# Weight parts, x and y at multiples of 512 bytes in SBUF, in a fused decoder layer on one core

## Chip, cores, metric

The kernel runs on one core of a Trainium2 chip. The metric is the device time of one execution in microseconds. PE, ACT, DVE, POOL and SP are the engines for matrix products, activations, vector operations, general work and DMA issues.

## What is computed

One decoder layer with four mixers, and a final RMSNorm:

```python
D_MODEL = 4096; SEQ = 256; DEPTH = 1; D_BRANCH = 1024
def hybrid_layer(x, norm_w, w_in, ..., w_out):
    h = rms_norm(x, norm_w)
    proj = jnp.einsum('bsd,de->bse', h, w_in)          # 4096 x 13328
    (rq, rk, rv, rg, mq, mk, mv, mg, sz, sxbc, sdt, lx, lg) = jnp.split(proj, ...)
    y_ret  = retention(rq, rk, rv, ret_gn_w) * silu(rg)
    y_moba = moba_attention(mq, mk, mv) * silu(mg)
    y_ssm  = mamba2_ssd(sz, sxbc, sdt, ...)
    y_lru  = rg_lru(lx, ...) * silu(lg)
    y = jnp.concatenate([y_ret, y_moba, y_ssm, y_lru], axis=-1)
    return x + jnp.einsum('bse,ed->bsd', y, w_out)     # 4096 x 4096
# then rms_norm(x, final_norm_w)
```

All inputs are float32. Each large product is made of three matmuls in the type float32r, from parts: an operand a is split into a high part (a rounded to float32r) and a low part (a minus the high part), and the kernel adds high x high, low x high and high x low.

## The kernel before, in words

**Chunks.** The weights come in chunks, as a rule two k-tiles (`KC = 2`, 256 rows of the weight) by 512 columns, in the order in which they are used. The columns of `w_in` are put into 25 groups (`GROUPS`). The first group has 1040 columns (`rv` and `sdt`) and is read one k-tile at a time, 32 chunks, each with the x rows it needs; the other 24 have 512 columns and 16 chunks each; the output projection has 8 column tiles of 512 and 16 chunks each. `load(n)` issues the DMA of chunk n on SP into one of four `raw` tiles (`RAW = 4` chunks ahead). `split(n)` (lines 145 to 160) makes `whi` on ACT (line 159) and `wlo` on DVE (line 160), two chunks ahead (`SPL = 2`), three tiles of each. For the last output tile some chunks are kept in six `hhi`/`hlo` tiles.

**Matmuls.** `products` (lines 669 to 674) makes three matmuls for one half e of the 256 rows: line 672 high x of the activations with `whi`, line 673 low x with `whi`, line 674 high x with `wlo`. The activations' parts are the weights that PE holds (128x128 out of a tile `xT` of 512 columns: high e=0, high e=1, low e=0, low e=1), and `whi`/`wlo` stream through as the moving operand, 512 columns at a time. In the first group each k-tile's 1040 columns are cut by `CUTS` into 504, 280 and 256 columns, in three pairs of accumulators (two `pm` pairs, one `pb` pair). The output projection does the same in `mms` (lines 727 to 735) with `yhl`, the split outputs of the mixers, in `xT` tiles too: per chunk of two k-tiles six matmuls for e=0 and then six for e=1. In the last output tile the second half of the rows is done in two halves of 256 columns.

**Everything between.** The mixers' own work is cut into short functions in a list, `todo`, and one of them (`slot()`) goes between two chunks. Their scratch tiles `t1` are six tiles of 512 columns that are handed out in turn. `softplus` (lines 261 to 275) has five small tiles of its own in the `const` pool, for `dt` (32 columns, in `ssd_dt`) and for `lam` (8 columns, in `lru_lam`). `lru_gate` (lines 493 to 510) multiplies split weights `lwh`, `lwl` (held by PE) with a split `r1` tile (moving), 12 matmuls of 256 columns for a pair of heads. A row of bf16 matmuls on a tile of zeros (line 659) runs at the start.

**Where tiles lie.** Pools are laid one behind the other along the bytes of a partition, in the order in which they are opened; a pool's tiles lie one behind the other, each of its own size. The `const` pool begins at byte 16512 and takes 7712, so `xT` begins at 24224, which is 160 past a multiple of 512; a tile of 2048 bytes keeps that offset. A `raw`, `whi` or `wlo` tile has 1040 columns (`RW`), 4160 bytes, which is 64 past a multiple of 512. By this and the new pools of the change, the offsets (address modulo 512) are:

| tile | before | with the change |
|---|---|---|
| `xT` (split x, later split y), each of its four parts | 160 | 0 |
| `whi`, three buffers, each of two k-tiles | 416, 480, 32 | 0, 0, 0 |
| `wlo`, three buffers | 96, 160, 224 | 0, 0, 0 |
| `whi` in the first group: second and third cut | whi + 480 and whi + 64 | 0 and 0 |
| `hhi`, `hlo`, `rs`, `fw`, `xres` | 448 (`rs` 288) | 0 |
| `raw`, four buffers | 160, 224, 288, 352 | 0, 64, 128, 192 |
| `lwh`, `lwl` of the gates | 384 | 352 |
| `r1` of the gates | 320 | 288 |
| `t1` | 320 | 288 |

The pairs `whi`/`wlo` are used in turn: 480/160, then 416/96, then 32/224.

Of the kernel before, what the change touches and what calls it, by code (L numbers as in the profile page):

```python
# [11 lines left out]
F32 = mybir.dt.float32  # L12
# [5 lines left out]
P = 128  # L18
# [3 lines left out]
KC = 2  # L22
XW = S + 1
SPL, RAW, HOLD, WARM = 2, 4, 6, 34
RW = 1040
CUTS = ((0, 504), (504, 784), (784, 1040))
NCH = KT // KC
EPS = 1e-6

# [27 lines left out]
NO = D // 512  # L57
# [34 lines left out]
def tile_kernel(ctx: ExitStack, tc: tile.TileContext, t: dict):  # L92
# [4 lines left out]
    cp = ctx.enter_context(tc.tile_pool(name="const", bufs=1))  # L97
    xp = ctx.enter_context(tc.tile_pool(name="xp", bufs=KT))
    wp = ctx.enter_context(tc.tile_pool(name="wp", bufs=1))
    pm = ctx.enter_context(tc.tile_pool(name="pm", bufs=4, space=PSUM))  # L100
    pb = ctx.enter_context(tc.tile_pool(name="pb", bufs=4, space=PSUM))
    br_stack = ExitStack()
    sp = br_stack.enter_context(tc.tile_pool(name="sp", bufs=2))
# [9 lines left out]
    for gi, (what, cols) in enumerate(GROUPS):  # L113
        w = len(cols)
# [10 lines left out]
    def b4():  # L125
        return br.tile([P, 4, S], F32, name="b4", bufs=4)

    def load(n):
        if n >= len(chunks):
            return  # L130
        where, src, kt, nk, w = chunks[n]
        raw = wp.tile([P, RW], F32, name="raw", bufs=RAW)
        if where == "x":
            c, k = divmod(kt, KC)
            xraws[n] = b4().rearrange("p a b -> p (a b)")
            nc.sync.dma_start(out=xraws[n][:, :XW], in_=t["xt"][c][:, k * XW:(k + 1) * XW])
        if n == 0:

            for i, (a, b) in enumerate(CUTS):
                (nc.sync if i else nc.scalar).dma_start(out=raw[:, a:b], in_=src[:, a:b])  # L140
        else:
            nc.sync.dma_start(out=raw[:, :nk * w], in_=src)
        raws[n] = raw

    def split(n):
        if n >= len(chunks):
            return
        where, _, kt, nk, w = chunks[n]
        if where == "x":
            split_x(xraws.pop(n))  # L150
        raw = raws.pop(n)
        c = kt // KC
        pool, tag, bufs, size = wp, "w", SPL + 1, RW
        if where == "last" and c % (SPL + 1 + HOLD) > SPL:
            pool, tag, bufs, size = holds[0], "h", HOLD, KC * 512
        hi = pool.tile([P, size], F32R, name=tag + "hi", bufs=bufs)
        lo = pool.tile([P, size], F32R, name=tag + "lo", bufs=bufs)
        for a, b in CUTS if n == 0 else ((0, nk * w),):
            A.copy(hi[:, a:b], raw[:, a:b])  # L159
            V.tensor_tensor(lo[:, a:b], raw[:, a:b], hi[:, a:b].bitcast(F32), ALU.subtract)  # L160
        parts[n] = (hi, lo)
# [5 lines left out]
    def pcol(name, i=0, n=1):  # L167
        return par[:, PCOL[name][0] + i:PCOL[name][0] + i + n]

    xT, holds = [], []  # L170

    def split_x(raw):
        x = xp.tile([P, 512], F32R, name="xT")
        r, g = raw[:, 0:S], raw[:, S:XW]
        A.activation(x[:, 0:256], r, AF.Copy, scale=g)  # L175
        V.scalar_tensor_tensor(x[:, 256:512], r, g, x[:, 0:256].bitcast(F32), op0=ALU.mult, op1=ALU.subtract)  # L176
        xT.append(x)
# [48 lines left out]
    st = {}  # L226

    def t1(name="t1"):
        return sp.tile([P, 512], F32, name="t1", bufs=6)

    lent = itertools.cycle([12, 14])

# [25 lines left out]
    def to_qk(tk, qk, u):  # L258
        A.copy(qk[:, 2 * u:2 * u + 2, :], turned(tk, u).rearrange("p (a b) -> p a b", a=2))

    def softplus(x, n, tag):

        a, e, s, q, p = (cp.tile([P, n], F32, name=f"sp_{tag}{i}") for i in range(5))
        V.scalar_tensor_tensor(a, x, -1.0, x, op0=ALU.mult, op1=ALU.min)
        A.activation(e, a, AF.Exp)
        V.tensor_scalar(s, e, 2.0, None, op0=ALU.add)
        V.reciprocal(s, s)
        V.tensor_tensor(s, s, e, ALU.mult)
        V.tensor_tensor(q, s, s, ALU.mult)
        V.tensor_scalar(p, q, 1.0 / 17, None, op0=ALU.mult)  # L270
        for k in range(15, 1, -2):
            V.scalar_tensor_tensor(p, p, 1.0 / k, q, op0=ALU.add, op1=ALU.mult)
        V.scalar_tensor_tensor(p, p, 1.0, s, op0=ALU.add, op1=ALU.mult)
        V.tensor_scalar(a, x, 0.0, None, op0=ALU.max)
        V.scalar_tensor_tensor(x, p, 2.0, a, op0=ALU.mult, op1=ALU.add)
# [27 lines left out]
    def norm_mm(hl, n):  # L303
        ps = pb.tile([P, 512], F32, name="pb")
        for k in range(2):
            T.matmul(ps[:, :n * S], ones_r, hl[k][:, :n * S], start=k == 0, stop=k == 1)
        r = t1()
        A.activation(r[:, :n * S], ps[:, :n * S], AF.Sqrt, bias=epsc[:, 0:1], scale=1.0 / 256)
        V.reciprocal(r[:, :n * S], r[:, :n * S])
        return r  # L310
# [81 lines left out]
    dt = cp.tile([P, 2, 16], F32, name="dt")  # L392
# [3 lines left out]
    selr = cp.tile([48, 16], F32R, name="selr")  # L396

    def ssd_dt():
        softplus(dt.rearrange("p a b -> p (a b)"), 32, "dt")
        V.memset(da, 0.0)  # L400
        ea = cp.tile([P, 16], F32, name="ea")
        A.activation(ea, pcol("alog", 0, 16), AF.Exp)
        for k in range(2):
            V.scalar_tensor_tensor(da[:, k, 0:16], dt[:, k, :], -1.0, ea, op0=ALU.mult, op1=ALU.mult)
            V.tensor_copy(da[:, k, 32:48], da[:, k, 0:16])
        V.tensor_copy(selr, con[0:48, C_SEL:C_SEL + 16])
# [63 lines left out]
    lam8 = cp.tile([P, 8], F32, name="lam8")  # L470

    def lru_lam():
        V.tensor_scalar(lam8, pcol("lam", 0, 8), -1.0, None, op0=ALU.mult)
        softplus(lam8, 8, "lam")
        V.tensor_scalar(lam8, lam8, -8.0, None, op0=ALU.mult)

    def lru_w(n):
# [60 lines left out]
    def after(what, ps):  # L538
        name, i = what
        if name == "rv":  # L540
            st["v"] = [br.tile([P, 1024], F32, name="v") for _ in range(2)]
            for j, (a, b) in enumerate(CUTS):
                n = min(b, 1024) - a
# [69 lines left out]
        elif name == "lx":  # L613
            tk = rows_of(ps)

            def f(e):
                n = 4 * i + e
                lru_w(n)
                conv(piece("lxT", e), "lcw", n, pcol("lcb", n), ych(Y_LRU + n))

            def both(*fs):
                for g in fs:
                    g()

            split, ugate, scan = ([lambda n=4 * i + e, g=g: g(n) for e in range(4)] for g in
                                  (lru_split, lru_gate, lru_scan))
            todo.extend([None, lambda: turn(tk, 0, "lxT"), lambda: f(0), lambda: f(1), lambda: turn(tk, 1, "lxT"),
                         lambda: both(split[0], split[1]), lambda: f(2), lambda: both(ugate[0], ugate[1]),
                         lambda: f(3), lambda: both(split[2], split[3]), None, lambda: both(ugate[2], ugate[3]), None,
                         lambda: both(scan[0], scan[1]), lambda: both(scan[2], scan[3])])  # L630
        else:
            base = {"sz": Y_SSM, "rg": Y_RET, "mg": Y_MOBA, "lg": Y_LRU}[name]
            todo.extend(gate(ps, base + 4 * i))
            if name == "sz" and i == 1:
                todo.append(None)
                norm_units(Y_SSM, "snw")
# [17 lines left out]
    for n in range(RAW):  # L654
        load(n)
# [4 lines left out]
    for n in range(SPL):  # L660
        split(n)
# [14 lines left out]
    n, c0, ps = 0, 0, None  # L676
    while chunks[n][0] in ("x", "in"):
        _, _, k0, nk, w = chunks[n]
        if k0 == 0:
# [3 lines left out]
            if c0 == 1:  # L683
                ps += [pb.tile([P, 512], F32, name="pb") for _ in range(2)]
        split(n + SPL)
        load(n + RAW)
        hi, lo = parts.pop(n)
        for k in range(nk):
            kt = k0 + k
            for j, (a, b) in enumerate(CUTS if c0 == 1 else ((0, w),)):  # L690
                for e in range(2):
# [27 lines left out]
    br_stack.close()  # L719
    fp = ctx.enter_context(tc.tile_pool(name="fp", bufs=1))  # L720
    holds.append(fp)
    rs = [fp.tile([P, D], F32, name=f"rs{k}") for k in range(2)]
    fss = fp.tile([P, 2, NO + 1], F32, name="fss")
    m = fp.tile([P, 2], F32, name="fm")
    fr = fp.tile([P, 2], F32, name="fr")

    def mms(ps, e, c, p, c0=0, c1=512):
        hi, lo = p
# [37 lines left out]
    for o in range(NO):  # L766
# [11 lines left out]
        for c in range(NCH):  # L778
            split(n + SPL)
            load(n + RAW)  # L780
            held[c] = parts.pop(n)
            mms(ps[0], 0, c, held[c])
            n += 1
            if c == NCH - 1:
                finish(o, 0, ps[0], xres[0], fw)
            if c >= lag:
                p = held.pop(c - lag)
                for a, b in ((0, 256), (256, 512)) if lag else ((0, 512),):
                    mms(ps[1 + a // 256], 1, c - lag, p, a, b)
# [59 lines left out]
```

## Time and profile before

| what | us |
|---|---|
| median of 3 runs (lowest, highest) | 1601.29 (1600.91, 1603.0) |
| profiled execution: its own time | 1602.49 |
| profiled execution: span from first to last instruction | 1600.7 |
| PE busy | 1586.9 |
| DVE busy | 856.8 |
| ACT busy | 749.2 |

The profile was taken in one execution. Its span goes from the first instruction to the last; the execution's own time is 1.8 us longer. A PE row of the timeline tells when a matmul starts and how long it lasts until its results are there; the next one starts before that, so the spacing of two starts is what a matmul costs on PE.

### The profile page before, as it was taken

Reading aid. Unit: us, or ns where it says so; the run is one execution under the profiler, and the core shown is the slowest. Engines: PE = TensorE matmul, PEld = TensorE weight load, DVE = VectorE, ACT = ScalarE, POOL = GpSimd, SP = SyncE. Lnnn points to the kernel's source line nnn. Section 1 sums busy time; section 2 is a strip of 40 time slices with the busy share of each in tenths; the row PEclk is TensorE's granted clock in tenths of the full one; section 3 lists DMA queues with packets and bytes.
Section 4 is the critical chain, followed back from the end, with each engine's and each line's share of the span. In section 5 each row is a group of like instructions: output and inputs, shape, how many; then the busy total and the mean of one; then the engine's idle time right before and its main releaser. Section 6 shows DMA issues by size and latency. Waiting matters only on the chain.

```text
span 1600.7 us, 19179 instructions
## 1 busy us (share of the span) xinstructions
PE 1586.9 (99%) x7356; PEld 1302.5 (81%) x7356; DVE 856.8 (54%) x1024; ACT 749.2 (47%) x936; POOL 19.2 (1%) x39
## 2 busy tenths in 40 slices
PE   9999999999999999999999999999999999999997
PEld 8988888888887778888888888888888888888886
DVE  5564444475556644444457667444456444545454
ACT  5654444454445434444448755433346334344441
POOL 0000000000000000000000000000000000000000
PEclk9999999999999999999999999999999999999999
DMA  8975454555554455545555455555555666666664
GB/s 282 300 248 184 171 174 174 176 178 191 172 184 171 148 181 185 171 171 179 181 193 173 169 194 175 191 187 186 185 184 184 230 210 209 212 206 212 207 223 145
DMA packets 90236, 308.03 MB, mean 192 GB/s; under 512 B 10272, under 2 KB 15904, under 8 KB 90144
## 3 DMA queue, kind: packets, MB, share of 16 engines
q1 hardware_dynamic: 86256, 296.85, 54.1%
q0 software_dynamic: 2304, 7.34, 1.7%
q10 hardware_dynamic: 1584, 2.62, 0.4%
q8 instruction: 57, 0.93, 0.2%
q14 instruction: 35, 0.29, 0.0%
HBM read 302.58 MB, written 4.19 MB: 192 GB/s over the span
## 4 chain that ended last, share of the span: by engine, by line
PE 98%; issue 1%; DMA 0%; DVE 0%; ACT 0%; SPq 0%; POOLq 0%; POOL 0%; DVEq 0%
PE pm L672 24%; PE pm L673 24%; PE pm L674 24%; PE pm L734 7%; PE pm L735 7%; PE pm L733 7%; PE pb L251 1%; PE pb L674 0%; PE pb L672 0%; PE pb L673 0%; DMA raw<-in_w 0%; PE pb L464 0%; PE pb L360 0%; PE pb L349 0%; PE pb L387 0%
## 5 line engine op out<-in xcount | busy, mean ns | idle before, releaser
L160 DVE TENSOR_TENSOR wlo<-raw,whi 128x1024 fp32r<-128x1024 f32 (+2 forms) x536 | 653.7, 1221 | 641.6 <-ACT whi L159 640.3
L159 ACT CAST whi<-raw 128x1024 fp32r<-128x1024 f32 (+2 forms) x536 | 559.3, 1045 | 746.1 <-PE pm L673 515.5
L672 PE MATMUL pm<-whi,xT 128*128 128x512 f32 (+2 forms) x1664 | 656.4, 394 | 1.9 <-ACT whi L159 1.9
L673 PE MATMUL pm<-whi,xT 128*128 128x512 f32 (+2 forms) x1664 | 649.4, 390 | 0.0
L674 PE MATMUL pm<-wlo,xT 128*128 128x512 f32 (+2 forms) x1664 | 648.0, 390 | 0.6 <-DVE wlo L160 0.6
L672 PEld LDWEIGHTS pm<-whi,xT 128*128 128x128 f32 x1664 | 313.2, 188 | 71.0 <-ACT whi L159 2.2
L674 PEld LDWEIGHTS pm<-wlo,xT 128*128 128x128 f32 x1664 | 313.1, 188 | 68.9 <-DVE wlo L160 1.0
L673 PEld LDWEIGHTS pm<-whi,xT 128*128 128x128 f32 x1664 | 313.2, 188 | 64.7
L734 PE MATMUL pm<-whi,xT 128*128 128x512 f32 (+1 forms) x484 | 188.3, 389 | 0.0
L735 PE MATMUL pm<-wlo,xT 128*128 128x512 f32 (+1 forms) x484 | 187.3, 387 | 0.0
L733 PE MATMUL pm<-whi,xT 128*128 128x512 f32 (+1 forms) x484 | 187.1, 387 | 0.0
L733 PEld LDWEIGHTS pm<-whi,xT 128*128 128x128 f32 x484 | 90.9, 188 | 20.5
L734 PEld LDWEIGHTS pm<-whi,xT 128*128 128x128 f32 x484 | 90.8, 188 | 19.8
L735 PEld LDWEIGHTS pm<-wlo,xT 128*128 128x128 f32 x484 | 90.9, 188 | 19.4
L243 ACT ACTIVATE y<-pm,rstd 128x512 f32<-128x512 f32 x24 | 16.6, 690 | 15.3 <-PE pm L674 15.3
L286 DVE SCALAR_TENSOR_TENSOR y<-pb,par,y 128x255 f32<-128x255 f32 (+2 forms) x48 | 23.0, 479 | 1.0
L175 ACT ACTIVATE xT<-b 128x256 fp32r<-128x256 f32 x32 | 15.5, 505 | 10.3 <-DMA b<-in_xt 10.3
L735 PE MATMUL pm<-hlo,xT 128*128 128x256 f32 (+1 forms) x60 | 19.1, 318 | 0.0
L734 PE MATMUL pm<-hhi,xT 128*128 128x256 f32 (+1 forms) x60 | 19.1, 318 | 0.0
L733 PE MATMUL pm<-hhi,xT 128*128 128x256 f32 (+1 forms) x60 | 19.1, 318 | 0.0
L176 DVE SCALAR_TENSOR_TENSOR xT<-b,xT 128x256 fp32r<-128x256 f32 x32 | 14.9, 480 | 7.7 <-ACT xT L175 7.7
L529 DVE TENSOR_TENSOR y<-y,pb 128x512 f32<-128x512 f32 x16 | 10.9, 686 | 13.9 <-PE pb L251 13.8
(193 smaller groups left out, 682.8 us busy)
## 6 DMA issues: line engine op xcount, KB each, us to landing
raw<-in_w SPq DMA_DIRECT2D x384, 512.0 KB, 3.5
raw<-in_wo SPq DMA_DIRECT2D x128, 512.0 KB, 4.2
raw<-in_w SPq DMA_DIRECT2D x31, 520.0 KB, 4.4
b<-in_xt SPq DMA_DIRECT2D x32, 128.5 KB, 4.3
b<-in_x SPq DMA_DIRECT2D x8, 512.0 KB, 5.9
xres<-in_x POOLq DMA_DIRECT2D x16, 256.0 KB, 6.4
fw<-in_fnw POOLq DMA_DIRECT2D x8, 256.0 KB, 5.4
out<-rs ACTq DMA_DIRECT2D x8, 256.0 KB, 3.4
```

The costliest lines, as they stand in the source:

```text
L159: A.copy(hi[:, a:b], raw[:, a:b])
L160: V.tensor_tensor(lo[:, a:b], raw[:, a:b], hi[:, a:b].bitcast(F32), ALU.subtract)
L175: A.activation(x[:, 0:256], r, AF.Copy, scale=g)
L243: A.activation(tk[k], ps[k], func, scale=rstd[:, k:k + 1])
L251: T.transpose(ps[:, e * S + k * P:e * S + (k + 1) * P], tk[k][:, (2 * u + e) * P:(2 * u + e + 1) * P], ident)
L286: V.scalar_tensor_tensor(out[:, d:S], src[:, 0:S - d], ww(k), out[:, d:S], op0=ALU.mult, op1=ALU.add)
L672: T.matmul(ps[:, :w], xh, hi[:, o:o + w], start=first, stop=False)
L673: T.matmul(ps[:, :w], xl, hi[:, o:o + w], start=False, stop=False)
L674: T.matmul(ps[:, :w], xh, lo[:, o:o + w], start=False, stop=last)
L733: T.matmul(ps[:, c0:c1], xh, hi[:, a:b], start=kt == 0, stop=False)
L734: T.matmul(ps[:, c0:c1], xl, hi[:, a:b], start=False, stop=False)
L735: T.matmul(ps[:, c0:c1], xh, lo[:, a:b], start=False, stop=kt == KT - 1)
```

## The change

It takes care of where tiles begin. `whi` and `wlo` get 1152 columns (`WW`, 4608 bytes, nine times 512) of which 1040 or 1024 are used; `raw`, whose rows stay at 4160 bytes, goes to a pool of its own behind them. A tile `pad` of 32 columns that nothing uses, and five small tiles of each `softplus` fewer, let the `const` pool end at a multiple of 512. `softplus` works in one `t1` tile instead, and there are five `t1` tiles where there were six. The cuts of the first group become 512, 256 and 272 columns, so that each begins at a multiple of 512 bytes. The small tiles of the final norm, `fss`, `fm` and `fr`, become parts of one tile `fsm` of 64 columns in front of `rs`.

```diff
-RW = 1040
-CUTS = ((0, 504), (504, 784), (784, 1040))
+RW, WW = 1040, 1152
+CUTS = ((0, 512), (512, 768), (768, 1040))
...
     wp = ctx.enter_context(tc.tile_pool(name="wp", bufs=1))
+    rp = ctx.enter_context(tc.tile_pool(name="rp", bufs=RAW))
...
-        raw = wp.tile([P, RW], F32, name="raw", bufs=RAW)
+        raw = rp.tile([P, RW], F32, name="raw")
...
-        pool, tag, bufs, size = wp, "w", SPL + 1, RW
+        pool, tag, bufs, size = wp, "w", SPL + 1, WW
...
     xT, holds = [], []
+    cp.tile([P, 32], F32, name="pad")
...
-        return sp.tile([P, 512], F32, name="t1", bufs=6)
+        return sp.tile([P, 512], F32, name="t1", bufs=5)
...
-    def softplus(x, n, tag):
+    def softplus(x, n):
 
-        a, e, s, q, p = (cp.tile([P, n], F32, name=f"sp_{tag}{i}") for i in range(5))
+        tmp = t1()
+        a, e, s, q, p = (tmp[:, i * n:(i + 1) * n] for i in range(5))
...
+    fsm = fp.tile([P, 64], F32, name="fsm")
+    fss = fsm[:, 0:2 * (NO + 1)].rearrange("p (a b) -> p a b", a=2)
+    m, fr = fsm[:, 32:34], fsm[:, 48:50]
     rs = [fp.tile([P, D], F32, name=f"rs{k}") for k in range(2)]
-    fss = fp.tile([P, 2, NO + 1], F32, name="fss")
-    m = fp.tile([P, 2], F32, name="fm")
-    fr = fp.tile([P, 2], F32, name="fr")
```

The scheduler puts some instructions in another order. On DVE, in the middle of the first group, the chain of `lru_lam`'s softplus (`sp_lam`, 8 columns) stood before, between the splits of that group's chunks (`wlo`) and of the x rows (`xT`):

```order
L473 TENSOR_SCALAR lam_111<-par 128x8
L264 SCALAR_TENSOR_TENSOR sp_lam_1399<-lam_111 128x8
L160 TENSOR_TENSOR wlo<-raw,whi 128x1040
L176 SCALAR_TENSOR_TENSOR xT<-b_462,xT 128x256
L266 TENSOR_SCALAR sp_lam_1401<-sp_lam_1400 128x8
L274 TENSOR_SCALAR sp_lam_1399<-lam_111 128x8
L267 RECIPROCAL sp_lam_1401<-sp_lam_1401 128x8
```

With the change it stands in the group after, on DVE among `ssd_dt`'s softplus of 32 columns, in two `t1` tiles (`t_1290` and `t_1399`), line numbers four higher from there on:

```order
L276 SCALAR_TENSOR_TENSOR t_1290<-t_1290 128x32
L270 TENSOR_SCALAR t_1399<-t_1399 128x8
L278 TENSOR_SCALAR t_1399<-lam_115 128x8
L276 SCALAR_TENSOR_TENSOR t_1290<-t_1290 128x32
L271 RECIPROCAL t_1399<-t_1399 128x8
L276 SCALAR_TENSOR_TENSOR t_1290<-t_1290 128x32
L272 TENSOR_TENSOR t_1399<-t_1399 128x8
```

The two chains were some 70 us apart and are now interleaved, before the `wlo` splits of the next chunks.

On PE, within one k-tile of the first group, the widths were these before (second row of the fence: the low part of x with `whi`; `pm` and `pb` are accumulators):

```order
L672 MATMUL pm<-whi,xT 128x504
L673 MATMUL pm<-whi,xT 128x504
L674 MATMUL pm<-wlo,xT 128x504
L672 MATMUL pm<-whi,xT 128x280
L673 MATMUL pm<-whi,xT 128x280
L674 MATMUL pm<-wlo,xT 128x280
L672 MATMUL pb<-whi,xT 128x256
L673 MATMUL pb<-whi,xT 128x256
```

and with the change:

```order
L676 MATMUL pm<-whi,xT 128x512
L677 MATMUL pm<-whi,xT 128x512
L678 MATMUL pm<-wlo,xT 128x512
L676 MATMUL pm<-whi,xT 128x256
L677 MATMUL pm<-whi,xT 128x256
L678 MATMUL pm<-wlo,xT 128x256
L676 MATMUL pb<-whi,xT 128x272
L677 MATMUL pb<-whi,xT 128x272
```

The number and the order of PE's instructions stay, and so does the sum of the columns.

## Rows read from the trace of the kernel before

**Rows 1.** The page, busy time of engines (share of the span, instructions); granted clock by slice.

```profile
PE 1586.9 (99%) x7356; PEld 1302.5 (81%) x7356; DVE 856.8 (54%) x1024; ACT 749.2 (47%) x936; POOL 19.2 (1%) x39
...
PEclk9999999999999999999999999999999999999999
```

**Rows 2.** The page, the chain that ended last, by engine.

```profile
PE 98%; issue 1%; DMA 0%; DVE 0%; ACT 0%; SPq 0%; POOLq 0%; POOL 0%; DVEq 0%
```

**Rows 3.** Waits of PE: who was waited for, us in total, times, longest.

```profile
PE pm L672 <- ACT whi L159: 1.9, 2, 1.2
...
PE pm L674 <- DVE wlo L160: 0.6, 1, 0.6
```

**Rows 4.** Groups by form: line, engine, out<-in, shapes, count | busy us, mean ns.

```profile
L672 PE MATMUL pm<-whi,xT 128*128 128x512 f32 x1536 | 612.0, 398 | 0.0
...
L734 PE MATMUL pm<-whi,xT 128*128 128x512 f32 x460 | 181.7, 395 | 0.0
...
L672 PE MATMUL pm<-whi,xT 128*128 128x504 f32 x64 | 25.5, 398 | 1.9 <-ACT whi L159 1.9
...
L672 PE MATMUL pm<-whi,xT 128*128 128x280 f32 x64 | 19.0, 296 | 0.0
...
L672 PE MATMUL pb<-whi,xT 128*128 128x256 f32 x64 | 18.0, 282 | 0.0
...
L734 PE MATMUL pm<-hhi,xT 128*128 128x256 f32 x40 | 11.2, 280 | 0.0
...
L734 PE MATMUL pm<-hhi,xT 128*128 128x512 f32 x20 | 7.9, 394 | 0.0
...
L734 PE MATMUL pm<-whi,xT 128*128 128x256 f32 x24 | 6.7, 281 | 0.0
```

**Rows 5.** Timeline of PE, three chunks of the output projection: start us, us, line.

```profile
1317.83 0.39 PE L733 MATMUL pm<-whi,xT 128*128 128x512 f32 x1
...
1319.69 0.40 PE L735 MATMUL pm<-wlo,xT 128*128 128x512 f32 x1
1319.93 0.39 PE L733 MATMUL pm<-whi,xT 128*128 128x512 f32 x1
...
1320.63 0.40 PE L733 MATMUL pm<-whi,xT 128*128 128x512 f32 x1
...
1323.40 0.39 PE L733 MATMUL pm<-whi,xT 128*128 128x512 f32 x1
...
1325.92 0.39 PE L735 MATMUL pm<-wlo,xT 128*128 128x512 f32 x1
1326.14 0.39 PE L733 MATMUL pm<-whi,xT 128*128 128x512 f32 x1
```

**Rows 6.** Timeline of PE, two calls of the gates: first and last of twelve.

```profile
843.07 0.28 PE L502 MATMUL pb<-r,lwh 128*128 128x256 f32 x1
...
844.37 0.28 PE L504 MATMUL pb<-r,lwl 128*128 128x256 f32 x1
...
855.58 0.28 PE L502 MATMUL pb<-r,lwh 128*128 128x256 f32 x1
...
856.82 0.28 PE L504 MATMUL pb<-r,lwl 128*128 128x256 f32 x1
```

**Rows 7.** Warm-up matmuls: all of line 659 (min/median/max ns); the last six merged.

```profile
L659 PE MATMUL pb<-v x34: 219/314/314, 1.0 to 4.1; 128*128 128x128 bf16 x34
...
3.83 0.50 PE L659 MATMUL pb<-v 128*128 128x128 bf16 x6
```

**Rows 8.** Timeline of PE, first group: first matmul of k-tiles three apart.

```profile
71.72 0.39 PE L672 MATMUL pm<-whi,xT 128*128 128x504 f32 x1
...
80.30 0.39 PE L672 MATMUL pm<-whi,xT 128*128 128x504 f32 x1
```

**Rows 9.** Line 272 on DVE, softplus of `lam`: duration ns min/median/max.

```profile
L272 DVE SCALAR_TENSOR_TENSOR sp_lam<-sp_lam,sp_lam x7: 161/167/170, 38.3 to 41.3; 128x8 f32<-128x8 f32 x7
```

More of the change, by code (lines that the diff above doesn't have):

```diff
@@ L398, in ssd_dt @@
     def ssd_dt():
-        softplus(dt.rearrange("p a b -> p (a b)"), 32, "dt")
+        softplus(dt.rearrange("p a b -> p (a b)"), 32)
         V.memset(da, 0.0)
@@ L473, in lru_lam @@
         V.tensor_scalar(lam8, pcol("lam", 0, 8), -1.0, None, op0=ALU.mult)
-        softplus(lam8, 8, "lam")
+        softplus(lam8, 8)
         V.tensor_scalar(lam8, lam8, -8.0, None, op0=ALU.mult)
```

## Prediction

> **What bounds the kernel now.** I read the page's busy table first, then the chain, then the waits of PE, and last the spacing of single matmuls. PE is busy 1586.9 of 1600.7 us, and its granted clock stands at 9 or more tenths in all 40 slices, the 2.4 GHz level [rows 1]. The chain that ended last is PE for 98% [rows 2]. PE waits for another engine almost nowhere: 1.9 us for the first `whi` and 0.6 us for a `wlo`, both at the start [rows 3]. So neither the loads nor ACT and DVE set the time; the number of matmuls times the spacing of their starts does. The mean duration in the groups (398 ns for 128x512) is no spacing, because consecutive matmuls overlap; spacing is read from start times in the timeline.
>
> In a stretch of the output projection 36 matmuls of 512 columns start between 1317.83 and 1326.14 us [rows 5]: 8.31 / 36 = 230.8 ns each. 512 columns at 2.4 GHz are 213.3 ns, so each pays 17.5 ns more. And the spacing goes by buffer: the three chunks of twelve matmuls take 2.80, 2.77 and 2.74 us, that is 233.3, 230.8 and 228.3 ns a matmul, with the same instructions, shapes and weights' offset. What differs is which of the three buffers `whi` and `wlo` lie in: offsets 480/160, 416/96 and 32/224 (address modulo 512, table above), while `xT` lies at 160 throughout. Single spacings in it run from 0.22 us (from 1325.92, `wlo` at 224) to 0.24 us (from 1319.69, `wlo` at 160, the offset of `xT` itself) [rows 5]. So addresses do count, by up to 9 ns a matmul below and above.
>
> **The change, part by part.**
>
> *The offsets.* The change puts both operands of all large matmuls at offset 0 (table above). What the spacing becomes there, no row shows directly. The nearest rows are those of the RG-LRU gates, lines 502 to 504: the one place where every matmul has its moving tile at one offset (320) and its weights at one offset (384), both multiples of 64. There the spacing locks: in the call at 855.58 us twelve matmuls of 256 columns run 11 steps in 1.24 us, 112.7 ns each; in the call at 843.07 us 11 steps take 1.30 us, 118.2 ns [rows 6]. Taken to 512 columns these are 225.5 and 236.4 ns: two locked spacings, one on each side of today's 230.8. The bounds from rows: below, a spacing with only the fixed cost of the bf16 warm-up matmuls. Six of them from 3.83 us span 0.50 us, the shortest lasting 219 ns, so (500 - 219) / 5 = 56 ns for 128 columns, 2.7 ns over 53.3 [rows 7]: 216.0 ns at 512 columns. Above, the 240 ns of the worst `wlo` step [rows 5].
>
> I take 226 ns. It is what the faster gate calls show, and what the best buffer pair already reaches in single steps [rows 5]; the offsets of today, 32 past a multiple of 64, make each row of an operand straddle one more boundary of 64, 128 and 256 bytes than it must, and that goes. That straddling costs time is an inference from the buffers' differences, no row isolates it.
>
> The terms, against the profiled execution's 1602.49 us:
> - 512 columns: 3 x (1536 + 460 + 20) = 6048 matmuls [rows 4], each 230.8 - 226 = 4.8 ns less: -29.0 us.
> - The first group, widths 504, 280, 256 now 512, 256, 272: 64 of each width and product [rows 4], the same 1040 columns, so no term of its own. Three k-tiles take 80.30 - 71.72 = 8.58 us [rows 8], 2.860 us each; 6 x 1040 columns at 226 / 512 ns are 2.754. 32 x 0.106 = -3.4 us.
> - The last output tile's halves, 3 x (40 + 24) = 192 matmuls of 256 columns [rows 4], 118 to 113 ns [rows 6]: -1.0 us.
> - `lru_lam`'s softplus moves on DVE from the first group into the next one (first pair of fences above): some 13 instructions of 128x8, 167 ns each in the median [rows 9], 2.2 us of DVE and one Exp on ACT, between the splits of three chunks. DVE is 54% busy [rows 1] and the splits run two chunks, 5.5 us, ahead of PE: 0 us. If that cover were gone, at most those 2.2 us once.
> - One `t1` fewer: each tile of `ssd_w` is now reused after five allocations, not six. `ssd_y` of the pair before has read it a whole slot, one chunk, earlier: 0 us. Without that cover the eight pairs would each wait up to a slot, 8 x 2.8 us; I give that no weight of its own, since the order of PE is unchanged.
> - `raw` in a pool of its own, the pad, the one tile `fsm` for three small ones, and the first `dm` load issued later on SP: the same loads, and the instructions of the tail wait for the same engines as before. 0 us.
>
> Sum: 1602.5 - 33.4 = 1569.1 us. The profiled execution lies 1.2 us above the median of the runs, 1601.29, so **1568 us** as a median.
>
> By row, then, an address is worth up to 5 ns a matmul either way [rows 5]. The Trainium skill speaks against it: "SBUF — State Buffer", section Specifications (TRN2), gives SBUF 16-byte lines, and its section on the bandwidth-pool intuition gives PE a second, independent read port for weights; all tiles begin at multiples of 32 already, so by these rules the change moves nothing and the time stays 1601 us. The trace agrees only in part: it has three spacings for three buffers that are all multiples of 16.
>
> **The rivals.**
>
> *Slower: equal offsets collide.* The price is the weights of the next matmul, loaded while the present one streams. If reads of the two streams that stand at one offset get in each other's way, the change makes that the case for every matmul. For it: the slowest buffer pair is the one whose `wlo` has `xT`'s own offset, 160, and the 240 ns step is such a product [rows 5]; and uniform offsets can lock at 118.2 ns per 256 columns [rows 6]. Against it: that chunk's mean is 233.3 all the same, so most of its twelve steps are well below 240, and a third of its products have this offset; and the two gate calls, alike in every offset, lock differently, so equal distances alone don't decide. At 236.4 ns: +5.6 x 6048 = 33.9, first group 32 x (6240 x 0.4617 - 2860) ns = +0.7: 1637 us (1636 as a median). At 233.3 it is +15.1 in the main term, 1618; at 240, +55.6, with 2.5 for the rest 1661. It decides from the point where the mean spacing passes 230.8.
>
> *No change: the offset of the start is not what counts.* Three buffers differ because of where they lie to each other, or to the accumulators, and the mean over three equal offsets is again some 231 ns: 1601 us. For it: on the mean of all buffers the excess is about the same in every stage (2.860 us for 6240 columns in the first group is 234.7 ns per 512). Against it: three buffers at one offset can hardly average out as three different ones do.
>
> *Much faster: the whole excess is straddling.* At 216.0 ns: -14.8 x 6048 = -89.5, first group 18 x 2.7 + 2600 = 2649 ns a k-tile, 32 x 0.211 = -6.8, halves -1.7: 1504.5, as a median 1503 us. Against it: the gate matmuls, on multiples of 64 with both operands, still pay 6 ns or more per 256 columns [rows 6], and bf16 rows [rows 7] move half the bytes.
> The Trainium skill's "TensorE: Matmul & The Clock Gate", section Back-to-back issue gap, has N / 2.4 + 2.5 ns, 215.8 at 512 columns, whatever the address; the warm-up rows agree with it (56 ns), the fp32r rows do not (230.8).
>
> **How the numbers follow.** Forecast (spacings of 225 to 229 ns, 1562 to 1590 us) 0.50; a spacing between that and 216, 0.08; no change 0.12; slower 0.30. The likeliest gives 1568. The range runs from 1548 to 1632: the low end takes in about half of the case beyond the forecast, the high end the slower case up to a spacing of some 235.5 ns; outside stay about 0.05 below and 0.12 above. A measurement of this kernel tells 0.2% (3.2 us, 0.5 ns of spacing) from no change. Faster by more than that: 0.58; within it 0.12; slower 0.30.
>
> **What would show it.** Right: the output projection's chunks of twelve all take the same time, about 2.71 us, whichever buffer; three k-tiles of the first group take 8.26 us; PE stays at 98% of the chain and still waits only at the start. Wrong: chunks alike but at 2.80 us or more (collision), chunks at 2.77 us or still unlike (the offset is not the cause), chunks near 2.59 us (all of it was straddling). New waits of PE on `wlo` in the second group, or of DVE on `t1` in the SSD pairs, would show that a cover failed.

## The result, and the profile after

| | before | with the change |
|---|---|---|
| median of 4 runs, us (lowest to highest) | 1601.10 (1600.32 to 1603.0) | 1578.33 (1577.83 to 1579.22) |
| ratio, 95% interval | | 0.9857 (0.984 to 0.9874) |
| span of the profiled execution, us | 1600.7 | 1576.9 |

The change makes the kernel 1.4% faster. The page of the changed kernel, as [rows 1, 2]: busy time, granted clock by slice, and the chain that ended last, by engine.

```profile
PE 1564.0 (99%) x7356; PEld 1299.7 (82%) x7356; DVE 855.6 (54%) x1024; ACT 749.8 (48%) x936; POOL 19.3 (1%) x39
...
PEclk9999999999999999999999999999999999999999
...
PE 98%; issue 1%; DVE 0%; DMA 0%; ACT 0%; SPq 0%; POOLq 0%; POOL 0%; DVEq 0%
```

PE's waits, as [rows 3]: who was waited for, us in total, times, longest.

```profile
PE pm L676 <- ACT whi L161: 1.3, 2, 0.6
...
PE pm L678 <- DVE wlo L162: 0.5, 1, 0.5
```

The span is 23.8 us shorter, and 22.9 of them are PE's own busy time, with the same instructions and no new wait. The moved softplus and the missing `t1` tile show no wait of PE. The timeline of PE (start us, us, line) shows where the time went. It has, in this order: two k-tiles of the first group three apart, as [rows 8]; the start of the second group; a chunk behind a slot, up to the next slot; the start of the output projection; three chunks of it, as [rows 5], and the start of the next output tile; one weight load; nine steps of the halves; the last matmul.

```profile
75.00 0.39 PE L676 MATMUL pm<-whi,xT 128*128 128x512 f32 x1
...
83.52 0.39 PE L676 MATMUL pm<-whi,xT 128*128 128x512 f32 x1
...
97.84 0.39 PE L676 MATMUL pm<-whi,xT 128*128 128x512 f32 x1
...
512.18 0.50 PE L676 MATMUL pm<-whi,xT 128*128 128x512 f32 x1
512.52 0.40 PE L677 MATMUL pm<-whi,xT 128*128 128x512 f32 x1
512.76 0.40 PE L678 MATMUL pm<-wlo,xT 128*128 128x512 f32 x1
...
515.17 0.38 PE L450 MATMUL pb<-csr,selr 48*128 48x256 f32 x1
...
1215.75 0.39 PE L737 MATMUL pm<-whi,xT 128*128 128x512 f32 x1
...
1303.86 0.39 PE L737 MATMUL pm<-whi,xT 128*128 128x512 f32 x1
...
1306.58 0.39 PE L737 MATMUL pm<-whi,xT 128*128 128x512 f32 x1
...
1309.30 0.39 PE L737 MATMUL pm<-whi,xT 128*128 128x512 f32 x1
...
1312.02 0.39 PE L737 MATMUL pm<-whi,xT 128*128 128x512 f32 x1
...
1347.38 0.39 PE L737 MATMUL pm<-whi,xT 128*128 128x512 f32 x1
...
1400.19 0.39 PE L739 MATMUL pm<-wlo,xT 128*128 128x512 f32 x1
1400.19 0.19 PEld L737 LDWEIGHTS pm<-whi,xT 128*128 128x128 f32 x1
...
1559.80 0.28 PE L737 MATMUL pm<-hhi,xT 128*128 128x256 f32 x1
...
1560.88 0.28 PE L737 MATMUL pm<-hhi,xT 128*128 128x256 f32 x1
...
1566.52 0.28 PE L739 MATMUL pm<-hlo,xT 128*128 128x256 f32 x1
```

The three chunks are alike, 2.72 us each, where they took 2.80, 2.77 and 2.74 [rows 5]; a whole output tile of 192 matmuls takes 1347.38 - 1303.86 = 43.52 us, 226.67 ns each. The same stage boundaries in the timeline of the kernel before (second group, output projection, last matmul):

```profile
100.30 0.40 PE L672 MATMUL pm<-whi,xT 128*128 128x512 f32 x1
...
1233.70 0.40 PE L733 MATMUL pm<-whi,xT 128*128 128x512 f32 x1
...
1590.02 0.27 PE L735 MATMUL pm<-hlo,xT 128*128 128x256 f32 x1
```

| stage | before, us | after, us | difference | forecast |
|---|---|---|---|---|
| up to the second group | 100.30 | 97.84 | -2.5 | -3.4 |
| 24 groups of the input, 4608 matmuls | 1133.40 | 1117.91 | -15.5 | -22.1 |
| output projection: 1440 of 512, 192 of 256 columns | 356.32 | 350.77 | -5.5 | -6.9 - 1.0 |
| sum | 1590.02 | 1566.52 | -23.5 | -33.4 |

### The profile page after: what moved, and what is told of

Its sections match the earlier page's. It is cut to its first block, busy times and chain, and to the rows that moved or that the text cites. A ratio compares the mean times of both kernels' runs of the same rounds, so it can differ in the third digit from the quotient of the medians.

```text
span 1576.9 us, 19178 instructions
## 1 busy us (share of the span) xinstructions
PE 1564.0 (99%) x7356; PEld 1299.7 (82%) x7356; DVE 855.6 (54%) x1024; ACT 749.8 (48%) x936; POOL 19.3 (1%) x39
## 4 chain that ended last, share of the span: by engine, by line
PE 98%; issue 1%; DVE 0%; DMA 0%; ACT 0%; SPq 0%; POOLq 0%; POOL 0%; DVEq 0%
PE pm L676 24%; PE pm L678 24%; PE pm L677 23%; PE pm L738 7%; PE pm L739 7%; PE pm L737 7%; PE pb L254 1%; PE pb L678 0%; PE pb L677 0%; PE pb L676 0%; DMA raw<-in_w 0%; PE pb L468 0%; PE pb L364 0%; PE pb L353 0%; PE pb L341 0%
## 5 line engine op out<-in xcount | busy, mean ns | idle before, releaser
L676 PE MATMUL pm<-whi,xT 128*128 128x512 f32 (+1 forms) x1664 | 652.2, 392 | 1.3 <-ACT whi L161 1.3
L678 PE MATMUL pm<-wlo,xT 128*128 128x512 f32 (+1 forms) x1664 | 642.5, 386 | 0.5 <-DVE wlo L162 0.5
L677 PE MATMUL pm<-whi,xT 128*128 128x512 f32 (+1 forms) x1664 | 641.3, 385 | 0.0
L738 PE MATMUL pm<-whi,xT 128*128 128x512 f32 (+1 forms) x484 | 185.9, 384 | 0.0
L739 PE MATMUL pm<-wlo,xT 128*128 128x512 f32 (+1 forms) x484 | 185.8, 384 | 0.0
L737 PE MATMUL pm<-whi,xT 128*128 128x512 f32 (+1 forms) x484 | 185.8, 384 | 0.0
L677 PE MATMUL pb<-whi,xT 128*128 128x272 f32 x64 | 18.4, 288 | 0.0
L678 PE MATMUL pb<-wlo,xT 128*128 128x272 f32 x64 | 18.4, 287 | 0.0
```

The source lines that it names most:

```text
L676: T.matmul(ps[:, :w], xh, hi[:, o:o + w], start=first, stop=False)
L677: T.matmul(ps[:, :w], xl, hi[:, o:o + w], start=False, stop=False)
L678: T.matmul(ps[:, :w], xh, lo[:, o:o + w], start=False, stop=last)
L737: T.matmul(ps[:, c0:c1], xh, hi[:, a:b], start=kt == 0, stop=False)
L738: T.matmul(ps[:, c0:c1], xl, hi[:, a:b], start=False, stop=False)
L739: T.matmul(ps[:, c0:c1], xh, lo[:, a:b], start=False, stop=kt == KT - 1)
```

## Experiments

"Own place" is the prediction's reason: an operand pays for where its own rows begin. "Distance" is its rival: what counts is how far the moving tile's address lies from the weights', whichever place both have. Pads between pools shift tiles; offsets are addresses modulo 512, distances are moving minus weights, modulo 256 unless said otherwise. Mean spacings are means over the steps between two 512-column matmuls, from the start times; steps over 0.3 us, nearly all of them the first behind other work on PE, are left out. In the sweeps the last output tile is left out, because its `hhi`/`hlo` tiles stay at 0. A spacing that repeats from step to step is called locked.

**Both at 32.**

```diff
-    cp.tile([P, 32], F32, name="pad")
+    cp.tile([P, 40], F32, name="pad")
...
+    pr.tile([P, 120], F32, name="padr")
```

> Weights (xT) and moving parts (whi, wlo) of the large matmuls all at 32 past a multiple of 512, everything else as in the changed kernel. Theory 'own place' (each operand pays when its rows straddle boundaries of 64 bytes and more): spacing of 512-column matmuls back to 230 to 232 ns, chunks of the output projection 2.77 us, 1597 to 1603 us. Rival 'distance' (only the distance between the two operands counts, and it is 0 as in the changed kernel): 226.7 ns, chunks 2.72 us, 1577 to 1580 us.

**Weights alone at 160.**

```diff
-    cp.tile([P, 32], F32, name="pad")
+    cp.tile([P, 72], F32, name="pad")
...
+    pw.tile([P, 88], F32, name="padw")
```

> Only the weights' tiles xT go back to 160 past a multiple of 512; the moving parts stay at 0. 'Own place', if the weights' reads pay as the moving ones do: 228 to 230 ns, 1585 to 1595 us; if only the moving operand's place counts: 226.7 ns, 1578 us. 'Distance' (now 352): another spacing than 226.7, as unlike as the three buffers of the kernel before were, 228 to 233 ns, 1585 to 1612 us.

**Moving parts alone at 32.**

```diff
+    pw.tile([P, 8], F32, name="padw")
...
+    pr.tile([P, 120], F32, name="padr")
```

> Only the moving parts go to 32 past a multiple of 512; the weights stay at 0. 'Own place': the moving reads straddle, 230 to 232 ns, 1595 to 1603 us, and at least as slow as the kernel with only the weights off. 'Distance' (now 32): 228 to 233 ns, 1585 to 1612 us, and no order between this kernel and that one.

Measured, each against the kernel before on the same chip (1601.39): both at 32, 1580.43 us (1578.89 to 1580.79), ratio 0.9865 (0.985 to 0.9879); weights at 160, 1614.87, 1.0081 (1.0066 to 1.0096); moving parts at 32, 1613.23, 1.0072 (1.0055 to 1.0088). Timelines of PE, first matmuls of output tiles, 192 matmuls apart. Both at 32:

```profile
1305.63 0.39 PE L739 MATMUL pm<-whi,xT 128*128 128x512 f32 x1
...
1349.15 0.39 PE L739 MATMUL pm<-whi,xT 128*128 128x512 f32 x1
```

Weights alone at 160:

```profile
1333.35 0.39 PE L739 MATMUL pm<-whi,xT 128*128 128x512 f32 x1
...
1378.15 0.39 PE L739 MATMUL pm<-whi,xT 128*128 128x512 f32 x1
```

Moving parts alone at 32:

```profile
1332.29 0.39 PE L741 MATMUL pm<-whi,xT 128*128 128x512 f32 x1
...
1377.09 0.39 PE L741 MATMUL pm<-whi,xT 128*128 128x512 f32 x1
```

That is 43.52 us with both at 32, exactly as with both at 0, and 44.80 us (233.3 ns a matmul) with either one moved alone. "Own place" falls: being off a multiple of 512, or of 64, costs nothing by itself, and an aligned moving tile is slower than the kernel before if the weights are elsewhere. "Distance" fits: with the weights at 160 it is 96, with the moving parts at 32 it is 32, and the sweep below, with the weights at 0, has 233.3 to 233.5 and 233.0 to 233.2 ns at these two. The 2 us of the first kernel over the changed one lie before the second group, which begins at 99.56 us instead of 97.84.

**All the rest of the change, at the old offsets.**

```diff
-RW, WW = 1040, 1152
-CUTS = ((0, 512), (512, 768), (768, 1040))
+RW, WW = 1040, 1040
+CUTS = ((0, 504), (504, 784), (784, 1040))
...
-    cp.tile([P, 32], F32, name="pad")
+    cp.tile([P, 72], F32, name="pad")
...
+    pw.tile([P, 64], F32, name="padw")
```

> All the rest of the change (five t1 tiles, softplus in a t1 tile, raw in its own pool, one fsm tile) with the offsets and cuts of the kernel before: xT 160, whi 32, 416, 480, wlo 96, 160, 224, paired 32/96, 416/160, 480/224. Both theories: 230 to 232 ns, 1598 to 1605 us, the gain gone. If the gain came from the rest: 1578 us.

1600.92 us, ratio 0.9999 (0.999 to 1.0008). The whole gain is in offsets and cuts. The expectation lists the pairs wrongly: they are 480/160, 416/96 and 32/224, as in the kernel before, and the `wlo` steps of three chunks in turn average 235.3, 231.0 and 225.9 ns in the output projection, where the kernel before has 235.5, 231.3 and 225.9.

**The old cuts alone.**

```diff
-CUTS = ((0, 512), (512, 768), (768, 1040))
+CUTS = ((0, 504), (504, 784), (784, 1040))
```

> The changed kernel with the first group's old cuts, 504, 280 and 256 columns, whose second and third begin 480 and 64 past a multiple of 512. If the cuts have a share in the gain: three k-tiles of the first group 8.58 us as before where the changed kernel has some 8.52, 1579 to 1581 us in all. If the place of the cuts counts nothing there: as the changed kernel, 1578 us. 512-column spacing behind the first group 227 ns either way.

1579.63 us (1578.73 to 1581.21), a range that overlaps the changed kernel's. Three k-tiles of the first group, in its timeline:

```profile
76.02 0.39 PE L676 MATMUL pm<-whi,xT 128*128 128x504 f32 x1
...
84.54 0.39 PE L676 MATMUL pm<-whi,xT 128*128 128x504 f32 x1
```

8.52 us, as with the new cuts (83.52 - 75.00 = 8.52). So the cuts show no share; what gain a k-tile has, 8.58 to 8.52, comes with the tiles' offsets. The 1.3 us between the medians lie before the second group again, which begins at 99.13 us.

**A sweep of the distance, by groups.**

```diff
+        if where != "x" and pool is wp:
+            o = SHIFT[(n - 32) // 16]
+            hi, lo = hi[:, o:o + nk * w], lo[:, o:o + nk * w]
```

`SHIFT` holds columns of 4 bytes, one entry for each group and output tile; the splits write there too.

> The changed kernel, but each group of columns after the first and each output tile begins at another place in its whi and wlo tiles, so that its distance to the weights (xT at 0) is another: 0, 32, 64, ... 480 bytes, then 16, 48, 80, 144, 272, 4, 8, 0 for the 24 groups of the input, and 64, 128, 192, 256, 320, 384, 448, 32 for the output tiles. 'Distance, zero only': 226.7 ns in steady stretches of the groups at 0, 230 to 235 ns at every other distance (32 as measured, 233.4), total 1605 to 1615 us. 'Distance, by lines' (what counts is the distance modulo 64 or 128 bytes): groups at every second or fourth step as good as 0, 226.7 ns, the others at 233, total 1594 to 1602 us. If some distance is better than 0, its groups show less than 226.7 ns.

1606.01 us (one run). Starts of the output tiles at distances 128, 192, 256, 320, 384 and 448 (not reduced):

```profile
1282.69 0.39 PE L742 MATMUL pm<-whi,xT 128*128 128x512 f32 x1
...
1327.30 0.39 PE L742 MATMUL pm<-whi,xT 128*128 128x512 f32 x1
...
1372.10 0.39 PE L742 MATMUL pm<-whi,xT 128*128 128x512 f32 x1
...
1415.64 0.40 PE L742 MATMUL pm<-whi,xT 128*128 128x512 f32 x1
...
1459.61 0.40 PE L742 MATMUL pm<-whi,xT 128*128 128x512 f32 x1
...
1504.23 0.40 PE L742 MATMUL pm<-whi,xT 128*128 128x512 f32 x1
```

By 192: 232.3, 233.3, 226.8, 229.0 and 232.4 ns, and the tile at 448 has 233.4 on the mean of its steps. 128 and 384 are alike, so are 192 and 448, and 256 is as good as 0: the period is 256 bytes. Within it neither expectation holds: 64 is between (228.9), every odd multiple of 32 gives 233.0 to 234.3, and 4 bytes off gives 236.7.

**Different distances for `whi` and `wlo`.** The same edit, with one entry of `SHIFT` for `whi` and one for `wlo`.

> The changed kernel with whi and wlo of a group at different distances from the weights (in bytes whi/wlo: 0/64, 0/128, 0/192, 64/0, 128/0, 192/0, all other pairs of multiples of 64, then pairs with multiples of 32 and of 16; three groups at 0/0 as control). Theory 'distance of the running stream to the weights loaded under it, modulo 256': a pair's mean spacing lies between the spacings of its two distances in the sweep (0: 226.7, 64: 228.9, 128: 232.4, 192: 233.3, odd multiples of 32: 233.3), with two thirds of the weight on whi: 0/64 227.5, 0/128 228.6, 64/0 228.2, 128/0 230.5. Rival 'the phase is carried from one matmul to the next': pairs come out off that line by over 1 ns, some possibly below 226.7 (0/0 would then not be the best), and a wlo at 64 behind a slower whi is quicker than at 64/64, as the 225 to 226 ns steps of the kernel before. Total 1600 to 1612 us.

1601.41 us (one run). Output tiles at 0/128, 128/0 and 0/192, and the start of the next:

```profile
1322.28 0.39 PE L744 MATMUL pm<-whi,xT 128*128 128x512 f32 x1
...
1367.07 0.39 PE L744 MATMUL pm<-whi,xT 128*128 128x512 f32 x1
...
1411.03 0.40 PE L744 MATMUL pm<-whi,xT 128*128 128x512 f32 x1
...
1455.02 0.40 PE L744 MATMUL pm<-whi,xT 128*128 128x512 f32 x1
```

233.3, 229.0 and 229.1 ns. By addition 0/128 should be 228.6 and 128/0 230.5; 0/64 measured 232.0 instead of 227.5. So the prices of two distances do not add up, and no pair came out below 226.7. A step's length hangs on the steps before it: the output tile at 64/0, just ahead of these, takes 231.1 ns a step, and in the kernel before the chunk of the same distances, 480/160 with `xT` at 160, takes 233.3 [rows 5] between chunks of other pairs.

**Another period, and the sixth `t1` tile.**

```diff
-RW, WW = 1040, 1152
+RW, WW = 1040, 1088
...
-        return sp.tile([P, 512], F32, name="t1", bufs=5)
+        return sp.tile([P, 512], F32, name="t1", bufs=6)
```

> The changed kernel with rows of 4352 bytes for whi and wlo (17 times 256) instead of 4608, so that their six buffers lie at 0 and 256 past a multiple of 512 by turns, and with six t1 tiles again, as the kernel before. 'Distance modulo 256': nothing changes, 226.7 ns in steady stretches, 1577 to 1580 us. If the period is 512, or if a change of distance between buffers costs as such: 229 ns or more, 1590 us or more. If the sixth t1 tile were worth something: under 1577 us.

1579.06 us (1578.61 to 1579.41). Steady output tiles take 43.52 us, so buffers at 0 and at 256 may alternate, rows of 4352 bytes do, and the sixth tile is worth nothing.

**Low parts of the weights in a tile of their own, at 128.** `xT` becomes a pair of tiles of 256 columns in two pools; `whi`, `wlo` and the high parts stay at 0.

```diff
-        x = xp.tile([P, 512], F32R, name="xT")
+        x, x2 = xp.tile([P, 256], F32R, name="xT"), xq.tile([P, 256], F32R, name="xL")
...
-        xh, xl = x[:, e * P:(e + 1) * P], x[:, 256 + e * P:256 + (e + 1) * P]
+        xh, xl = x[0][:, e * P:(e + 1) * P], x[1][:, e * P:(e + 1) * P]
```

> The weights' low parts go to a tile of their own, 128 bytes past a multiple of 512; high parts, whi and wlo stay at 0. So of three matmuls (high x whi, low x whi, high x wlo) one differs: the first by the weights that are loaded while it streams, the second by the weights it holds. In the pairs run 0/128 the third differed, with mean steps of 230.0 (first), 236.0 (second), 234.0 ns (third). 'The load under the stream counts': the same three, one place on, first 234, second 230, third 236 ns, mean 233.3. 'The weights in use count': first 236, second 234, third 230 ns. Either way 1608 to 1614 us. 'Only whi and wlo count': 226.7, 1578 us.

1600.61 us (one run): a miss for all three. A steady output tile, its first matmul and that of the next:

```profile
1321.65 0.40 PE L742 MATMUL pm<-whi,xT 128*128 128x512 f32 x1
...
1366.03 0.40 PE L742 MATMUL pm<-whi,xT 128*128 128x512 f32 x1
```

Its three steps average 232.3, 234.3 and 226.7 ns (64 of each), mean 231.1. That only `whi` and `wlo` count is refuted, since the weights of one product in three undo the gain. But neither "the load under the stream" (234, 230, 236) nor "the weights in use" (236, 234, 230) gives this pattern. Which of the reads meet stays open.

**A second sweep.** The first sweep's edit with other entries.

> The sweep again at 31 more distances (all other multiples of 8 from 24 to 248 bytes, and 12, 20, 28, 60, 68, 124, 132, 188, 196, 236, 244, 252), and 256 as control. By the first sweep 256 gives 226.8 ns, and all others lie between 228 and 237, none below 226.7; 60 and 68 close to 64's 228.9 if lines of 64 bytes matter, at 233 or more if only the exact distance does. One below 226 ns would be a better place than the change's.

1610.84 us (one run). Its timeline: the groups at 28, 60 and 68, and the output tile at 132 with the start of the next.

```profile
1104.77 0.40 PE L680 MATMUL pm<-whi,xT 128*128 128x512 f32 x1
...
1149.21 0.39 PE L680 MATMUL pm<-whi,xT 128*128 128x512 f32 x1
...
1193.65 0.40 PE L680 MATMUL pm<-whi,xT 128*128 128x512 f32 x1
...
1239.95 0.40 PE L741 MATMUL pm<-whi,xT 128*128 128x512 f32 x1
1285.05 0.40 PE L741 MATMUL pm<-whi,xT 128*128 128x512 f32 x1
...
1331.11 0.40 PE L741 MATMUL pm<-whi,xT 128*128 128x512 f32 x1
```

The groups take 44.44, 44.44 and 46.30 us, the output tile at 132 46.06 (239.9 ns). A miss again: 28, 60 and 252 are as good as 0, and 120, 132 and 244 are worse than anything before. Both sweeps together, mean ns a step of the group or tile:

| ns | distances in bytes |
|---|---|
| 226.7 to 227.0 | 0, 28, 60, 252 (and 256) |
| 228.9 to 231.2 | 12, 56, 64, 80, 112, 124, 188, 236, 248 |
| 231.7 to 234.4 | 8, 16, 24, 32, 40, 48, 88, 96, 104, 128, 136, 144, 152, 160, 168, 176, 184, 192, 196, 200, 208, 216, 224, 232 |
| 235.3 to 239.9 | 4, 20, 68, 72, 120, 132, 240, 244 |

A group of the input, with slots between its chunks, can read higher than an output tile: 256 has 226.8 as an output tile and 228.4 as a group, and a second group at 0 has 227.4. So a difference of 1 or 2 ns between two groups says little. Of the 64 multiples of 4 bytes in the period, 19 were not swept.

**The two other good distances through the whole kernel.**

```diff
+        if pool is wp:
+            hi, lo = hi[:, 15:15 + nk * w], lo[:, 15:15 + nk * w]
```

> The changed kernel with whi and wlo used from column 15 on, so that all large matmuls have the distance 60, one of those that the second sweep showed at 226.74 ns (the hold tiles of the last output tile stay at 0). 'Several distances lock at the same spacing, so equal offsets are nothing special': 226.7 ns in steady stretches, 1574 to 1582 us; under 1577 if it locks sooner behind a slot than distance 0 does (the changed kernel's input groups lose some 1.0 ns a matmul there, 4.6 us), over 1580 if later. If 60 is good only in that one group: 230 ns or more, 1595 us or more.

The same with 7 in place of 15:

> The same with column 7, distance 28 (226.76 ns in the second sweep, between 24 with 233.3 and 32 with 233.2). Same theory, same numbers: 226.7 ns in steady stretches, 1574 to 1582 us, and 20 us less than the kernel with the distance 32, 4 bytes further. If spacing goes by places of 32 bytes or more, as 'own place' would have it: 233 ns, 1613 us as at 32.

Distance 60: 1574.64 us (1574.33 to 1576.16), ratio to before 0.9831 (0.9816 to 0.9846). Distance 28: 1573.58 (1572.38 to 1575.56), 0.9826 (0.9809 to 0.9843). None of the four runs of either reaches the changed kernel's lowest, 1577.83. On the medians 28 is the better one, 4.8 us under the changed kernel, but its range overlaps that of 60. Timeline of PE at distance 28: three k-tiles of the first group, a chunk behind the same kind of slot as above, and a steady output tile.

```profile
82.46 0.39 PE L678 MATMUL pm<-whi,xT 128*128 128x512 f32 x1
...
90.84 0.39 PE L678 MATMUL pm<-whi,xT 128*128 128x512 f32 x1
...
509.58 0.50 PE L678 MATMUL pm<-whi,xT 128*128 128x512 f32 x1
509.92 0.39 PE L679 MATMUL pm<-whi,xT 128*128 128x512 f32 x1
510.15 0.39 PE L680 MATMUL pm<-wlo,xT 128*128 128x512 f32 x1
...
512.50 0.38 PE L452 MATMUL pb<-csr,selr 48*128 48x256 f32 x1
...
1298.27 0.39 PE L739 MATMUL pm<-whi,xT 128*128 128x512 f32 x1
...
1341.79 0.39 PE L739 MATMUL pm<-whi,xT 128*128 128x512 f32 x1
```

The steady tile takes 43.52 us again. The difference is behind the slots: at distance 28 the second step is already 0.23 us and the chunk takes 512.50 - 509.58 = 2.92 us; at distance 0 the first steps are 0.34 and 0.24 us and the chunk takes 515.17 - 512.18 = 2.99. The mean over the input's groups is 226.7 ns at 28 and 227.6 at 0, 4.1 us for 4608 matmuls; the three k-tiles take 8.38 us instead of 8.52.

## Why the prediction was right, and where its reason was not

**What held.** PE's spacing is the whole matter; it became uniform, three chunks alike at 2.72 us against 2.71 forecast; PE stays at 98% of the chain, with no new wait. The terms set at nothing (softplus, `t1`, `raw`'s pool, `pad`, `fsm`) are nothing together: 1600.92 with the old offsets.

**The reason that fell.** The step "the offsets of today, 32 past a multiple of 64, make each row of an operand straddle one more boundary ... and that goes" is wrong. Both operands at 32 give 226.67 ns, one alone at 32 or 160 gives 233.3. What the change does is to make the distance of the two operands 0 for every matmul, and 0 is one of the few good distances: 33 of the 45 swept are slower than today's 230.8. So 226 was near, but not for the reason given: the gate calls it was read from have the distance 192, which at 512 columns gives 233.3. That the figure taken from them lay so near the measured one was luck. The prediction also read rows 5 as 9 ns either way of the mean; the steps from 1325.92 and 1319.69 are 226 and 240 ns, 5 below and 9 above.

**The slower rival had the right quantity and the wrong sign.** "Equal offsets collide" rested on `wlo` at 160, `xT`'s own offset, being the slowest. In the kernel before, its steps (distance 0) average 234.7 ns and those of `wlo` at 224 (distance 64) 227.2; in kernels of one distance it is 226.7 and 228.9. The pairs show why: in a mixture a step carries what the steps before left, so a mean by buffer was no price of that buffer's place. The rival's price exists, 240 ns, but at 120, 132 and 244.

**The no-change rival** fell with the three equal chunks, and the much faster one too: no swept distance locks below 226.67 ns. The Trainium skill's "SBUF — State Buffer" (Specifications (TRN2), and the bandwidth-pool intuition), by whose lines of 16 bytes and independent weight port the prediction had a time of 1601, does not agree with these runs: 24, 28 and 32 bytes give 233.3, 226.8 and 233.2 ns, and moving the weights alone costs 1614.87 - 1578.33 = 36.5 us. The Trainium skill's "TensorE: Matmul & The Clock Gate", Back-to-back issue gap, has 215.8 ns at 512 columns by its formula for the isolated gap; no swept distance gives a mean under 226.7.

**The sizes.** 33.4 us were forecast, 23.5 came between the two profiles; the medians moved by 22.8 where 33.3 were forecast.
- The input's 512-column matmuls: forecast 4608 x 4.8 = 22.1, measured 15.5. The lock is 226.67, not 226 (-3.1). Behind each slot some 4 to 10 steps of 224 to 240 ns pass until it locks, which the prediction did not see, and which lift the groups' mean to 227.64 (-4.5). The mean before was 231.05, not 230.8 (+1.1).
- The output projection: 1440 steps of 231.17 became 226.94, -6.1 against -6.9. The halves went the other way: 117.46 to 119.57 ns on the mean, +0.4 where -1.0 was forecast. They lock at (1560.88 - 1559.80) / 9 = 120.0 ns, 13.3 over the 106.7 of 256 columns at 2.4 GHz. That is the excess that a 512-column matmul has too (226.7 - 213.3); scaling the excess by columns was the failing step.
- The first group: three k-tiles 8.52 us instead of the forecast 8.26, so 32 x 0.02 = 0.6 us; three widths by turns never come to one spacing at distance 0. The other 1.8 us before the second group are not shown to be the offsets' work: they lie for the most part in the first two k-tiles (9.56 us before, 7.51 after), and the kernel with the old offsets and cuts reaches the second group at 98.55 us, the one with both operands at 32 only at 99.56.

**What stays open.** Why 0, 28, 60 and 252 are good and 4, 68, 120, 132 and 244 bad. That the reads of the next weights meet the moving stream is argued from the rows, not shown: the weight load for the next matmul starts with the present one, both at 1400.19 us in the timeline above; no run could take the loads away, and the one with the low parts apart fitted neither form of this theory.

## What to carry to other kernels

Where PE is the bound and float32r matmuls, each with weights of its own, follow each other without a break, read the spacing of their starts by buffer, and treat the distance between the moving and the held operand in SBUF, modulo 256 bytes, as a parameter: one kernel that gives each group of columns its own distance sweeps it in a single run (differences of 1 or 2 ns need a whole kernel). Make it the same for all matmuls, and then choose it: between the best and the worst distance lie 13 ns of 227 here. A mean by buffer in a mixed sequence does not tell what that buffer's place is worth.

## What was not expected of the hardware

- Three steady spacings lie evenly apart: 226.67 (0 and 28), 233.33 (32) and 239.9 ns (132), that is 13.3, 20.0 and 26.6 over 213.3. Others come back too, such as 228.9 at 64.
- 4 bytes decide: 24, 28 and 32 give 233.3, 226.8 and 233.2 ns, 60, 64 and 68 give 226.7, 228.9 and 236.6; the period is 256 bytes.
- How soon PE comes back to its lock behind other work hangs on the distance: at 28 nearly always within two matmuls behind the first, at 0 after 4 to 10, with the same steady spacing.
